# A hybrid decoder block: split float32r products replaced by single float32 products, and the experts' ring filled earlier

## The chip, the cores and the metric

The kernel runs on one core of a Trainium2 chip. The metric is the device time of one execution in microseconds (us). In the views, PE is the matrix engine and PEld its weight loads, DVE the vector engine, ACT the scalar engine, POOL the general-purpose one, and SP the engine whose queue issues most transfers.

## The reference

One decoder block over 16 meta tokens and 512 tokens of width 1024, in float32. Cut to what matters:

```python
u = rms_norm(h, norm_mix_w)                                  # 528 x 1024
q_a, k_a, v_a, f_a, q_h, f_h, i_h, g_h, gate_a, gate_h = split(u @ w_in)
# attention, 8 heads of 64: logit[t,s] = q_t.k_s/8 + c_t - c_s, c = cumsum(log_sigmoid(f_a))
y_a = softmax(masked logits) @ v_a, then @ w_attn_out        # 512 -> 1024
# HGRN2, 8 heads of 128: S_t = diag(f_t) S_{t-1} + k_t v_t^T, o_t = S_t^T q_t
y_h = (rms_norm(o) * sigmoid(g_h)) @ w_hgrn_out              # 1024 -> 1024
h = h + (sigmoid(gate_a) * y_a + sigmoid(gate_h) * y_h) @ w_o
v = rms_norm(h, norm_ffn_w)
# experts: best of 4 groups, best 2 of the 8 experts in it, gate = softmax weights
h = h + sum over chosen experts of gate * ((silu(a) * b) @ w_e_out[e]),  a, b = split(v @ w_e_in[e])
out = rms_norm(h, norm_final_w)[16:]
```

There are 32 experts with 1024 x 1024 weights in and 512 x 1024 out, 201 MB in all, and every one of them is read.

## The kernel before, in words

**Projections.** The normalised input lies transposed in `u`, 8 blocks of 128 rows by 528 columns, and is kept as two float32r tiles, `uh` (the rounded value) and `ul` (what the rounding left). A weight tile of 128 output columns (8 x 128 x 128) is loaded as float32 by `fetch`, half a transfer of 1 MB at a time, and `cut` splits it into `wh` (ACT, line 158) and `wl` (DVE, line 159). `mm3` then makes three products for each of the 8 blocks: `wh` with `uh`, `wh` with `ul`, `wl` with `uh`; the fourth, low with low, is left out. Where the meta tokens are needed (`proj(True)`: forget gate and values of HGRN2, keys and values of attention) the 528 columns are done as two halves of 264; otherwise as 512. The order is: 8 heads of HGRN2 with four tiles each, 8 tiles of `w_gh`, 8 of `w_ho` (on `ohT_h`, `ohT_l`), 4 pairs of attention heads with three tiles each, 8 tiles of `w_ga` (the attention gates), 8 half-long tiles of `w_ao` (on `oaT_h`, `oaT_l`), and `w_o` in `part` (on `mixh`, `mixl`).

**Side work.** After each of the 8 blocks `stage.step()` lets a generator (`hgrn`, `attend`) put its next few instructions between the products, so that scans, softmax and transposes run beside the projections. In `attend` a score block is one product of high parts stacked over 128 rows (line 684) and one of 66 rows that carries the low parts and the forget bias (line 685).

**Transfers.** SP issues its transfers in program order. `weights` asks for loads up to three ahead of the current tile. 16 tiles (`SLOTS`) of a pool serve all big buffers and 5 more (`STREAM`) the weights and their splits. A transfer into a tile waits until the last reader of the tile's previous owner is done, and what follows it on SP waits too.

**Experts.** Experts p and p + 16 make a pair; its weights come as 12 chunks of 1 MB, 192 in all. 18 chunks (`RING`) are kept ahead through `ahead`, two more (`LOOSE`) lie in small buffers. In `first`, rows gathered for the pair (64 for each expert) meet the weights in float32, the two experts in the two halves of the array's columns (line 1126); SiLU; transposes; in `second` the product with the second weights (line 1166). The result `py` is split into `yh` and `yl` (lines 1170, 1171), and `scatter` multiplies both by the one-hot `PT` (lines 1212, 1213), 128x512 each, and adds `gate` times the sum to `x`. The second half of a pair's scatter runs between the transposes and the second product of the next pair (`fill`). Chunks are first asked for in the loop over `w_o`, after its first half.

Of the kernel before, what the change touches and what calls it, by code (L numbers as in the profile page):

```python
# [9 lines left out]
F32R = mybir.dt.float32r  # L10
# [18 lines left out]
SLOTS = 16  # L29
STREAM = 5  # L30
# [7 lines left out]
SHARED = (9, 10, 11, 16, 17)  # L38
# [26 lines left out]
def hybrid_block(tc, I, out, dbg=None):  # L65
# [3 lines left out]
    with ctx:  # L69
# [8 lines left out]
        def slot(name, n=4, dt=F32, w=None, stream=False):  # L78

            t_ = sb.tile([128, SLOT], dt, tag="stream" if stream else "slot", bufs=STREAM if stream else SLOTS, name=name)  # L80
            w = w or {4: L, 2: 1024, 1: 2048}[n]
            return t_[:, :n * w].rearrange("p (n w) -> p n w", n=n)
# [106 lines left out]
        ys, y2, sums, pvs, us = {}, {}, {}, {}, {}  # L189
# [29 lines left out]
        def fa(b):  # L219

            n, _, c0 = rows[b]
            o = pf[b // 2 if b > 0 else 0][:, c0 % 272:c0 % 272 + n]
            for i in range(2):
                for g in range(4):
                    T.matmul(o[32 * g:32 * g + 32], wfa[:, 4 * i + g], us[b, i][:, g], start=(i == 0), stop=(i == 1))

        def sw(b, i):
            n, _, c0 = rows[b]
            u = us[b, i] = slot("u")[:, :, :n]
            V.tensor_tensor(u, pvs[b, i], nmw[:, 4 * i:4 * i + 4, None].to_broadcast([128, 4, n]), op=ALU.mult)  # L230

        def hi(b, i):
            n, _, c0 = rows[b]
            A.activation(uh[i][:, :, c0:c0 + n], us[b, i], AF.Copy)

        def lo(b, i, eng):
            n, _, c0 = rows[b]
            eng.tensor_tensor(ul[i][:, :, c0:c0 + n], us[b, i], uh[i][:, :, c0:c0 + n].bitcast(F32), op=ALU.subtract)

        with tc.manual_schedule(engines={getattr(mybir.EngineType, e) for e in ("PE", "DVE", "Activation", "Pool")}):  # L240
# [23 lines left out]
            hi(-1, 0)  # L264
            hi(-1, 1)
            lo(-1, 0, G)
            lo(-1, 1, G)
# [4 lines left out]
            hi(0, 0)  # L272
            lo(0, 0, G)
            dg(2)
            sw(1, 0)
            ms(3)
            hi(0, 1)
            lo(0, 1, G)
            hi(1, 0)
            fa(0)  # L280
            tr(2, 0)
            lo(1, 0, G)
            cut(0)
            sw(1, 1)
            dg(3)
            tr(2, 1)
            hi(1, 1)
            lo(1, 1, G)
            fa(1)
            sw(2, 0)  # L290
            tr(3, 0)
            sw(2, 1)
            hi(2, 0)
            hi(2, 1)
            tr(3, 1)
            lo(2, 0, G)
            fa(2)
            sw(3, 0)
            sw(3, 1)
            hi(3, 0)  # L300
            hi(3, 1)
            lo(3, 0, G)
            fa(3)
            lo(2, 1, V)
            lo(3, 1, V)
        cut(1)
# [13 lines left out]
        def weights():  # L320
# [1055 lines left out]
```

## Time and profile before

| | us |
|---|---|
| median of 3 runs (1096.1 to 1099.58) | 1098.77 |
| the profiled execution | 1096.76 |
| its span, first to last instruction | 1094.8 |
| PE busy in it | 1047.2 |
| weight loads (PEld) busy | 689.2 |
| DVE busy | 575.0 |
| ACT busy | 329.5 |

Matmuls are pipelined and the ends of their records are modelled, so that a busy PE may still wait for up to the tail of a record. The windows end with the granted clock, the mean busy share of the transfer engines and GB/s. A matmul's form gives the array's part in use (rows * columns) and the moving operand; a float32r matmul is listed as f32 too. A row of the timeline or of the chain with a count covers that many instructions from the first one's start to the last one's end.

### The profile page before, as it was taken

How to read it: one execution, taken by the hardware profiler on the slowest of the kernel's cores; microseconds unless marked ns; L12 is line 12 of the kernel's file. 1: busy time of each engine (PE TensorE's matmuls, PEld its weight loads, DVE VectorE, ACT ScalarE, POOL GpSimd, SP SyncE). 2: the span in 40 equal slices, each digit the busy share in tenths (PEclk: the TensorE clock that was granted, in tenths of full speed). 3: DMA queues.
4: the chain of work that ended last, by engine and by line, in shares of the span. 5: the costliest groups of instructions: out<-in, count | busy, mean ns of one | idle time of the engine just before them, and what ended most of it. 6: DMA issues, size and time to landing. Idle time of an engine off the chain costs nothing.

```text
span 1094.8 us, 16543 instructions
## 1 busy us (share of the span) xinstructions
PE 1047.2 (96%) x6756; PEld 689.2 (63%) x6757; DVE 575.0 (53%) x1269; ACT 329.5 (30%) x643; POOL 67.7 (6%) x88
## 2 busy tenths in 40 slices
PE   9999999999999999999999999999999999988984
PEld 8888988988888898777788634333443333333331
DVE  6967877677633466666653533333443333323324
ACT  5545655555551243344434300000000000000003
POOL 5000000000000121100000000000000000000002
PEclk9999999999999999999999999999999999999997
DMA  6211221121222211221287999999999999999993
GB/s 221 95 44 74 78 78 43 75 79 40 78 86 89 96 59 59 79 77 39 77 323 299 321 419 419 418 419 420 419 418 420 419 419 420 420 420 418 420 415 127
DMA packets 41139, 255.61 MB, mean 233 GB/s; under 512 B 6143, under 2 KB 6399, under 8 KB 12000
## 3 DMA queue, kind: packets, MB, share of 16 engines
q1 hardware_dynamic: 37328, 248.39, 57.3%
q0 software_dynamic: 2416, 3.98, 1.0%
q10 hardware_dynamic: 1312, 2.11, 0.5%
q8 instruction: 55, 0.90, 0.3%
q14 instruction: 28, 0.23, 0.1%
HBM read 254.15 MB, written 4.19 MB: 236 GB/s over the span
## 4 chain that ended last, share of the span: by engine, by line
PE 60%; DMA 32%; DVE 4%; issue 1%; ACT 1%; POOL 0%; DVEq 0%; SPq 0%; ACTq 0%; POOLq 0%
DMA ch<-w_e 30%; PE pj L344 24%; PE py L344 6%; PE pk L344 5%; PE phu L1126 4%; PE pye L1166 4%; PE pd L561 1%; PE ph L1026 1%; PE pu L215 1%; PE ph L1024 1%; PE poa L712 1%; PE ph L1025 1%; PE pout L1212 1%; DMA xslot<-rows_of,xslot 1%; DMA rows_of<-v 1%
## 5 line engine op out<-in xcount | busy, mean ns | idle before, releaser
L344 PE MATMUL pj<-uh,ws 128*128 128x512 f32 (+1 forms) x928 | 295.0, 363 | 1.6 <-DVE ws L159 1.1
L1126 PE MATMUL phu<-ch,xslot 128*64 128x512 f32 x1024 | 232.6, 598 | 20.7 <-DMA ch<-w_e 20.7
L344 PEld LDWEIGHTS pj<-uh,ws 128*128 128x128 f32 x928 | 174.8, 189 | 27.3 <-issue 2.0
L1126 PEld LDWEIGHTS phu<-ch,xslot 128*64 128x64 f32 x1024 | 68.1, 136 | 175.9 <-issue 113.0
L344 PE MATMUL pj<-ul,ws 128*128 128x512 f32 (+1 forms) x464 | 164.1, 354 | 0.0
L1139 DVE TENSOR_TENSOR hs<-hs,phu 128x512 f32<-128x512 f32 x16 | 11.0, 688 | 208.6 <-PE phu L1126 191.4
L159 DVE TENSOR_TENSOR ws<-w,ws 128x1024 fp32r<-128x1024 f32 (+1 forms) x84 | 98.0, 1168 | 34.3 <-ACT ws L158 34.1
L1166 PE MATMUL pye<-ch,hs 128*64 128x512 f32 x512 | 113.9, 596 | 1.6 <-DVE hs L1152 1.1
L158 ACT ACTIVATE ws<-w 128x1024 fp32r<-128x1024 f32 (+1 forms) x83 | 84.2, 1015 | 54.0 <-PE py L344 40.3
L344 PE MATMUL pk<-uh,ws 128*128 128x264 f32 x352 | 95.4, 285 | 0.0
L344 PEld LDWEIGHTS pj<-ul,ws 128*128 128x128 f32 x464 | 87.4, 188 | 9.5 <-issue 0.2
L1214 DVE SCALAR_TENSOR_TENSOR x<-pout,gate,x 128x512 f32<-128x512 f32 x128 | 87.1, 742 | 1.1 <-PE pout L1213 1.1
L1138 ACT ACTIVATE hs<-phu 128x512 f32<-128x512 f32 x16 | 9.6, 597 | 254.6 <-PE phu L1126 254.6
L1166 PEld LDWEIGHTS pye<-ch,hs 128*64 128x64 f32 x512 | 35.1, 137 | 71.5 <-issue 64.6
L1170 ACT ACTIVATE yh<-pye 128x512 fp32r<-128x512 f32 x32 | 19.1, 598 | 163.2 <-PE pye L1166 163.2
L344 PEld LDWEIGHTS pk<-uh,ws 128*128 128x128 f32 x352 | 66.4, 189 | 0.6
L1171 DVE TENSOR_TENSOR yl<-pye,yh 128x512 fp32r<-128x512 f32 x32 | 22.1, 692 | 70.3 <-ACT yh L1170 68.7
L1212 PE MATMUL pout<-yh,PT 128*128 128x512 f32 x128 | 57.0, 445 | 0.0
L1213 PE MATMUL pout<-yl,PT 128*128 128x512 f32 x128 | 50.5, 395 | 0.2 <-DVE yl L1171 0.2
L344 PE MATMUL pk<-ul,ws 128*128 128x264 f32 x176 | 50.0, 284 | 0.0
L1212 PEld LDWEIGHTS pout<-yh,PT 128*128 128x128 f32 x128 | 24.0, 187 | 27.4 <-issue 13.8
L344 PE MATMUL py<-ohh,ws 128*128 128x512 f32 x128 | 40.3, 394 | 0.0
(323 smaller groups left out, 1520.7 us busy)
## 6 DMA issues: line engine op xcount, KB each, us to landing
ch<-w_e SPq DMA_DIRECT2D x189, 1024.0 KB, 20.0
w<-w_h SPq DMA_DIRECT2D x16, 1024.0 KB, 5.1
w<-w_gh SPq DMA_DIRECT2D x4, 1024.0 KB, 4.9
w<-w_ho SPq DMA_DIRECT2D x4, 1024.0 KB, 4.9
w<-w_a SPq DMA_DIRECT2D x4, 1024.0 KB, 5.0
w<-w_ga SPq DMA_DIRECT2D x4, 1024.0 KB, 4.9
w<-w_o SPq DMA_DIRECT2D x4, 1024.0 KB, 4.8
x<-x SPq DMA_DIRECT2D x4, 512.0 KB, 5.2
```

Of the source, the lines that this page charges most:

```text
L158: a = A.activation(wh, w, AF.Copy)
L159: b = V.tensor_tensor(wl, w, wh.bitcast(F32), op=ALU.subtract)
L215: T.matmul(pvs[b, i][:, k], rows[b][1][:, 512 * i + 128 * k:512 * i + 128 * k + 128], dgs[b], start=True, stop=True)
L344: T.matmul(p[i], a[:, k], m(k, i), start=(k == 0 and j == 0), stop=(k == nk - 1 and j == 2))
L1126: T.matmul(ph[n][r], x_[k // 4][:, k % 4, r], w[2 * e + n], start=(k == 0), stop=(k == KD - 1))
L1139: V.tensor_tensor(hs, hs, ph[1], op=ALU.mult)
L1166: T.matmul(py[n][r], hs[:, 128 * k + 64 * e:128 * k + 64 * e + 64], w[2 * (k % 2) + e], start=(k == 0), stop=(k == 3))
L1170: A.activation(yh[n], py[n], AF.Copy)
L1171: V.tensor_tensor(yl[n], py[n], yh[n].bitcast(F32), op=ALU.subtract)
L1212: T.matmul(po, PT[:, tb], yh[n], start=True, stop=False)
L1213: T.matmul(po, PT[:, tb], yl[n], start=False, stop=True)
L1214: V.scalar_tensor_tensor(x[tb][:, c], po, gate[:, tb, p:p + 1], x[tb][:, c], op0=ALU.mult, op1=ALU.add)
```

## The change

Every product of split operands becomes one product of plain float32 operands. `cut`, the high and low tiles and the instructions that make them go. `mm3` (three products) becomes `mm` (one), and the order of the normalisation's steps at the start is rewritten without the splits. A score block is one product of 65 rows: 64 of the head and one for the bias; `X` moves into `Y`'s tile. `scatter` is one product for each of 4 row blocks and half. `part` reads `mix` itself. The two pools of 16 and 5 tiles become one of 21. The chunks' loads begin one each after gates 2 to 8, then one after every second tile of `w_ao`, then the rest of the first 18 in the loop over `w_o`. The branch for experts with more than 64 rows changes in the same way.

```diff
-SLOTS = 16
-STREAM = 5
+SLOTS = 21
-SHARED = (9, 10, 11, 16, 17)
+EARLY = [i for i in range(20) if i not in LOOSE]
...
-            if i < len(loads) and ("l", i) not in made:
-                w = slot("w", 1, stream=True)[:, 0]
-                nc.sync.dma_start(w[:, :loads[i][1]], loads[i][0])
-                made["l", i] = w
-
-        def cut(i):
-            if i >= len(tiles) or ("s", i) in made:
-                return
-            li, o, c = tiles[i]
-            fetch(li)
-            w = made["l", li][:, o:o + c]
-            ws = slot("ws", 2, F32R, stream=True)
-            wh, wl = ws[:, 0, :c], ws[:, 1, :c]
-            if i == 0:
-                V.tensor_copy(wh, w)
-            else:
-                a = A.activation(wh, w, AF.Copy)
-            b = V.tensor_tensor(wl, w, wh.bitcast(F32), op=ALU.subtract)
-            if i == 1:
-                tc.keep_in_program_order(a)
-                tc.keep_in_program_order(b)
-            made["s", i] = [m.rearrange("p (k c) -> p k c", c=128 if c > 256 else 32) for m in (wh, wl)]
+            if i < len(loads) and i not in made:
+                made[i] = slot("w", 1)[:, 0]
+                nc.sync.dma_start(made[i][:, :loads[i][1]], loads[i][0])
...
-        uh = [slot(f"uh{i}", 4, F32R) for i in range(2)]
-        ul = [slot(f"ul{i}", 4, F32R) for i in range(2)]
+        u = [slot(f"u{i}", 4) for i in range(2)]
...
         def sw(b, i):
             n, _, c0 = rows[b]
-            u = us[b, i] = slot("u")[:, :, :n]
-            V.tensor_tensor(u, pvs[b, i], nmw[:, 4 * i:4 * i + 4, None].to_broadcast([128, 4, n]), op=ALU.mult)
-
-        def hi(b, i):
-            n, _, c0 = rows[b]
-            A.activation(uh[i][:, :, c0:c0 + n], us[b, i], AF.Copy)
-
-        def lo(b, i, eng):
-            n, _, c0 = rows[b]
-            eng.tensor_tensor(ul[i][:, :, c0:c0 + n], us[b, i], uh[i][:, :, c0:c0 + n].bitcast(F32), op=ALU.subtract)
+            V.tensor_tensor(u[i][:, :, c0:c0 + n], pvs[b, i], nmw[:, 4 * i:4 * i + 4, None].to_broadcast([128, 4, n]),
+                            op=ALU.mult)
...
-            fetch(tiles[i][0])
-            cut(i)
+            li, o, c = tiles[i]
+            fetch(li)
             if i + 1 < len(tiles):
                 for j in range(AHEAD + 1):
                     fetch(tiles[i + 1][0] + j)
-                cut(i + 1)
-            return made.pop(("s", i))
-
-        def mm3(p, wh, wl, mh, ml, nk, apart=False):
-
-            if apart:
-                for i in range(len(p)):
-                    for j, (a, m) in enumerate(((wh, mh), (wl, mh), (wh, ml))):
-                        for k in range(nk):
-                            T.matmul(p[i], a[:, k], m(k, i), start=(k == 0 and j == 0), stop=(k == nk - 1 and j == 2))
-                return
-            for ii in [range(len(p))]:
+            w = made[li][:, o:o + c]
+            if i + 1 == len(tiles) or tiles[i + 1][0] > li:
+                made[li] = None
+            return w.rearrange("p (k c) -> p k c", c=128)
+
+        def mm(p, w, m, nk, apart=False):
+
+            for i in range(len(p)) if apart else (0,):
                 for k in range(nk):
-                    for j, (a, m) in enumerate(((wh, mh), (wh, ml), (wl, mh))):
-                        for i in ii:
-                            T.matmul(p[i], a[:, k], m(k, i), start=(k == 0 and j == 0), stop=(k == nk - 1 and j == 2))
-                    stage.step()
+                    for j in (i,) if apart else range(len(p)):
+                        T.matmul(p[j], w[:, k], m(k, j), start=(k == 0), stop=(k == nk - 1))
+                    if not apart:
+                        stage.step()
 
         def proj(full):
-            wh, wl = weights()
+            w = weights()
             if full:
-                n = wh.shape[-1]
-                p = [bank("pj", True)[:n], bank("pk", True)[:n]]
-                mm3([a[:, 0:264] for a in p], wh, wl, lambda k, i: uh[k // 4][:, k % 4, 264 * i:264 * i + 264],
-                    lambda k, i: ul[k // 4][:, k % 4, 264 * i:264 * i + 264], KD, state["n"] <= 2)
-                return [a[:, 0:264] for a in p]
+                p = [bank("pj", True)[:, 0:264], bank("pk", True)[:, 0:264]]
+                mm(p, w, lambda k, i: u[k // 4][:, k % 4, 264 * i:264 * i + 264], KD, state["n"] <= 2)
+                return p
             p = bank("pj", True)
-            mm3([p], wh, wl, lambda k, i: uh[k // 4][:, k % 4, M:], lambda k, i: ul[k // 4][:, k % 4, M:], KD)
+            mm([p], w, lambda k, i: u[k // 4][:, k % 4, M:], KD)
...
-            V.scalar_tensor_tensor(oo, pt, hnw, g, op0=ALU.mult, op1=ALU.mult)
-            A.activation(ohT_h[h // 4][:, h % 4], oo, AF.Copy)
-            V.tensor_tensor(ohT_l[h // 4][:, h % 4], oo, ohT_h[h // 4][:, h % 4].bitcast(F32), op=ALU.subtract)
+            V.scalar_tensor_tensor(ohT[h // 4][:, h % 4], pt, hnw, g, op0=ALU.mult, op1=ALU.mult)
...
-                        T.matmul(p_[:, :n], X[h][0][:, r], Y[:, 2 * h, kk], start=True, stop=False)
-                        T.matmul(p_[:, :n], X[h][1][0:66, r], Y[0:66, 2 * h + 1, kk], start=False, stop=(k0 + n <= P))
+                        T.matmul(p_[:, :n], X[h][0:65, r], Y[0:65, h, kk], start=True, stop=(k0 + n <= P))
...
-            Y = slot("Y", 4, F32R)
-            X = [[piece(f"X{h}{j}", F32R, S) for j in range(2)] for h in range(2)]
+            Y = slot("Y", 4)
+            X = [Y[:, 2 + h, :S] for h in range(2)]
             for h in range(2):
                 r = slice(64 * h, 64 * h + 64)
-                nc.gpsimd.dma_start(Y[64:66, 2 * h + 1], chl[2 * pr + h:2 * pr + h + 1])
-                V.tensor_scalar(X[h][1][64:66], mhalf[64:66, 0:1].to_broadcast([2, S]), 2.0, None, op0=ALU.mult)
-                both(lambda o, i_: A.activation(o, i_[r], AF.Copy), Y[0:64, 2 * h], pk)
-                for i in range(2):
-                    o = slice(264 * i, 264 * i + 264)
-                    V.tensor_tensor(Y[0:64, 2 * h + 1, o], pk[i][r], Y[0:64, 2 * h, o].bitcast(F32), op=ALU.subtract)
-                G.tensor_copy(Y[64:128, 2 * h], Y[0:64, 2 * h].bitcast(F32))
+                nc.gpsimd.dma_start(Y[64:65, h], cfs[2 * pr + h:2 * pr + h + 1])
+                V.tensor_scalar(X[h][64:65], mhalf[64:65, 0:1].to_broadcast([1, S]), 2.0, None, op0=ALU.mult)
+                both(lambda o, i_: A.activation(o, i_[r], AF.Copy), Y[0:64, h], pk)
             pq = proj(False)
             for h in range(2):
-                r = slice(64 * h, 64 * h + 64)
-                A.activation(X[h][0][0:64], pq[r], AF.Copy, scale=0.125)
-                V.scalar_tensor_tensor(X[h][0][64:128], pq[r], 0.125, X[h][0][0:64].bitcast(F32), op0=ALU.mult, op1=ALU.subtract)
-                G.tensor_copy(X[h][1][0:64], X[h][0][0:64].bitcast(F32))
+                A.activation(X[h][0:64], pq[64 * h:64 * h + 64], AF.Copy, scale=0.125)
...
             logistic(ga[d], [pg])
+            if d:
+                ahead(EARLY[d - 1])
         stage.drain()
         if dbg:
-            nc.sync.dma_start(dbg["oa"], oaT_h.bitcast(F32))
-        mhl = [slot(f"mhl{b}", 2, F32R) for b in range(NB)]
-        mixh, mixl = ([m[:, j].rearrange("p (d t) -> p d t", d=KD) for m in mhl] for j in range(2))
+            nc.sync.dma_start(dbg["oa"], oaT)
         for d in range(KD):
-            wh, wl = weights()
+            w = weights()
             p = bank("py", True)
-            mm3([p], wh, wl, lambda k, i: oaT_h[:, k], lambda k, i: oaT_l[:, k], 4)
+            mm([p], w, lambda k, i: oaT[:, k], 4)
             g, t = ga[d], mix[d // 4][:, d % 4]
             V.tensor_tensor(g, p, g, op=ALU.mult)
             V.tensor_tensor(t, t, g, op=ALU.add)
-            for b in range(NB):
-                tt = t[:, 128 * b:128 * b + 128]
-                A.activation(mixh[b][:, d], tt, AF.Copy)
-                V.tensor_tensor(mixl[b][:, d], tt, mixh[b][:, d].bitcast(F32), op=ALU.subtract)
+            if d % 2:
+                ahead(EARLY[7 + d // 2])
...
-            cc = slice(512 * (k % 2), 512 * (k % 2) + 512)
-            a, b_ = (z_.rearrange("p k c -> p (k c)")[:, cc] for z_ in ab)
-            mh, ml = mixh[tb][:, k], mixl[tb][:, k]
-            T.matmul(p, mh, a, start=(k == 0), stop=False)
-            T.matmul(p, ml, a, start=False, stop=False)
-            T.matmul(p, mh, b_, start=False, stop=(k == KD - 1))
+        def part(p, tb, k, w):
+            T.matmul(p, mix[k // 4][:, k % 4, 128 * tb:128 * tb + 128],
+                     w.rearrange("p k c -> p (k c)")[:, 512 * (k % 2):512 * (k % 2) + 512],
+                     start=(k == 0), stop=(k == KD - 1))
...
-            for i in (*range(6), 8, 9, 10):
+            for i in EARLY[11:14]:
...
-            for i in (11, 12, 13):
+            for i in EARLY[14:16]:
...
-                ahead(tb + 13)
                 normal(tb - 1)
                 route(tb - 1)
 
             tb = NB - 1
-            ahead(tb + 14)
-            for i in (18, 19):
+            for i in EARLY[16:]:
...
-                A.activation(yh[n], py[n], AF.Copy)
-                V.tensor_tensor(yl[n], py[n], yh[n].bitcast(F32), op=ALU.subtract)
+                A.activation(y[n], py[n], AF.Copy)
...
-            PT, yh, yl = Y[p]
+            PT, y = Y[p]
             c = slice(512 * n, 512 * n + 512)
             for tb in range(NB):
                 po = bank("pout")
-                T.matmul(po, PT[:, tb], yh[n], start=True, stop=False)
-                T.matmul(po, PT[:, tb], yl[n], start=False, stop=True)
+                T.matmul(po, PT[:, tb], y[n], start=True, stop=True)
                 V.scalar_tensor_tensor(x[tb][:, c], po, gate[:, tb, p:p + 1], x[tb][:, c], op0=ALU.mult, op1=ALU.add)
```

## Rows read from the trace of the kernel before

**Rows 1.** The page's 40 slices: PE's busy tenths, and what transfers moved.

```profile
PE   9999999999999999999999999999999999988984
...
GB/s 221 95 44 74 78 78 43 75 79 40 78 86 89 96 59 59 79 77 39 77 323 299 321 419 419 418 419 420 419 418 420 419 419 420 420 420 418 420 415 127
```

**Rows 2.** Windows: length; busy us (count) of PE, PEld, DVE, ACT, POOL; clock; transfers.

```profile
33.00:618.10 585.10, 581.09 (x4424) 494.73 (x4424) 370.85 (x880) 271.56 (x537) 30.81 (x39) 1.00 0.29 100
618.10:1094.80 476.70, 436.12 (x2045) 166.67 (x2044) 179.94 (x332) 39.10 (x73) 23.05 (x23) 0.99 0.97 399
...
672.90:699.50 26.60, 26.60 (x130) 10.61 (x130) 10.79 (x20) 1.79 (x3) 0.99 (x1) 1.00 1.01 418
726.00:1062.00 336.00, 314.79 (x1463) 117.67 (x1464) 120.82 (x210) 19.72 (x33) 9.89 (x10) 1.00 1.01 419
```

**Rows 3.** PE's waits from 33.0 to 618.1: us, times, longest; six entries.

```profile
PE prk L872 <- DVE ob L866: 1.6, 3, 0.7
PE pj L344 <- DVE ws L159: 1.1, 1, 1.1
...
```

**Rows 4.** The chain in order of time: start, us, what.

```profile
300.56 22.94 PE pj L344 x99
323.51 44.80 PE py L344 x192
```

**Rows 5.** Timeline of SP's queue before the experts: the chunks' loads.

```profile
555.76 54.98 SPq L928 DMA_DIRECT2D ch<-w_e  x18
```

**Rows 6.** PE's groups by form: count, busy us, mean ns of one.

```profile
L1126 PE MATMUL phu<-ch,xslot 128*64 128x512 f32 x1024 | 232.6, 598 | 20.7 <-DMA ch<-w_e 20.7
L344 PE MATMUL pj<-uh,ws 128*128 128x512 f32 x576 | 198.2, 404 | 1.6 <-DVE ws L159 1.1 <-issue 0.5
...
L344 PE MATMUL pk<-uh,ws 128*128 128x264 f32 x352 | 95.4, 285 | 0.0
...
L225 PE MATMUL pf<-u,wfa 128*32 128x128 f32 x64 | 2.6, 279 | 0.0
```

**Rows 7.** Timeline: the second pair's first product, and one step's weight loads.

```profile
646.13 13.95 PE L1126 MATMUL phu<-ch,xslot 128*64 128x512 f32 x64
646.61 0.14 PEld L1126 LDWEIGHTS phu<-ch,xslot 128*64 128x64 f32 x2 [0.28 <-issue]
```

**Rows 8.** Timeline of PE at the start.

```profile
18.50 0.86 PE L225 MATMUL pf<-u,wfa 128*32 128x128 f32 x24
...
19.30 0.39 PE L338 MATMUL pj<-uh,ws 128*128 128x264 f32 x1
...
28.73 2.13 PE L338 MATMUL pk<-uh,ws 128*128 128x264 f32 x16
...
33.39 0.73 PE L344 MATMUL pj<-uh,ws 128*128 128x512 f32 x2 [1.10 <-DVE ws L159]
```

**Rows 9.** The page's costliest groups: two of DVE.

```profile
L159 DVE TENSOR_TENSOR ws<-w,ws 128x1024 fp32r<-128x1024 f32 (+1 forms) x84 | 98.0, 1168 | 34.3 <-ACT ws L158 34.1
...
L1214 DVE SCALAR_TENSOR_TENSOR x<-pout,gate,x 128x512 f32<-128x512 f32 x128 | 87.1, 742 | 1.1 <-PE pout L1213 1.1
```

**Rows 10.** Timeline of DVE at the start.

```profile
14.01 1.23 DVE L159 TENSOR_TENSOR ws<-w,ws 128x1024 fp32r<-128x1024 f32 x1
```

**Rows 11.** Timeline of PE in the second pair: scatter's groups and what follows them.

```profile
661.40 0.48 PE L1212 MATMUL pout<-yh,PT 128*128 128x512 f32 x1
...
663.73 7.09 PE L1166 MATMUL pye<-ch,hs 128*64 128x512 f32 x32
670.75 0.51 PE L1212 MATMUL pout<-yh,PT 128*128 128x512 f32 x1
...
672.79 0.65 PE L1126 MATMUL phu<-ch,xslot 128*64 128x512 f32 x2
```

**Rows 12.** Timeline of PE at the end: the last pair's second product, in two pieces.

```profile
1067.08 5.37 PE L1166 MATMUL pye<-ch,hs 128*64 128x512 f32 x24
...
1073.96 1.94 PE L1166 MATMUL pye<-ch,hs 128*64 128x512 f32 x8
```

More of the change, by code (lines that the diff above doesn't have):

```diff
@@ L76, in st, with slot @@
             return sb.tile(shape, dt, tag=tag or name, bufs=bufs, name=name or tag)
-        def slot(name, n=4, dt=F32, w=None, stream=False):
-            t_ = sb.tile([128, SLOT], dt, tag="stream" if stream else "slot", bufs=STREAM if stream else SLOTS, name=name)
+        def slot(name, n=4, dt=F32, w=None):
+            t_ = sb.tile([128, SLOT], dt, tag="slot", bufs=SLOTS, name=name)
             w = w or {4: L, 2: 1024, 1: 2048}[n]
@@ L391, in hybrid_block @@
         V.tensor_tensor_scan(cf, zero1[:8].to_broadcast([8, L]), z, 0.0, op0=ALU.add, op1=ALU.add)
-        chl = inside(cc, 2 * L, F32R).rearrange("p (j t) -> p j t", j=2)[0:8]
-        V.tensor_copy(chl[:, 0], cf)
-        V.tensor_tensor(chl[:, 1], cf, chl[:, 0].bitcast(F32), op=ALU.subtract)
+        cfs = inside(cc, L)[0:8]
+        V.tensor_copy(cfs, cf)
         if dbg:
@@ L407, in hybrid_block @@
         V.tensor_scalar(lb[:, 1], lb[:, 0], -1.0, 1.0, op0=ALU.mult, op1=ALU.add)
-        ohT_h = [slot(f"ohh{i}", 4, F32R, S) for i in range(2)]
-        ohT_l = [slot(f"ohl{i}", 4, F32R, S) for i in range(2)]
+        ohT = [slot(f"oh{i}", 4, F32, S) for i in range(2)]
         sT = [inside(ca, S).rearrange("p (c t) -> p c t", c=NB) for i in range(2)]
@@ L628, in hybrid_block @@
             for i in range(2):
-                nc.sync.dma_start(dbg["ohn"][i], ohT_h[i].bitcast(F32))
+                nc.sync.dma_start(dbg["ohn"][i], ohT[i])
         for d in range(KD):
-            wh, wl = weights()
+            w = weights()
             p = bank("py", True)
-            mm3([p], wh, wl, lambda k, i: ohT_h[k // 4][:, k % 4], lambda k, i: ohT_l[k // 4][:, k % 4], KD)
+            mm([p], w, lambda k, i: ohT[k // 4][:, k % 4], KD)
             V.tensor_tensor(mix[d // 4][:, d % 4], p, mix[d // 4][:, d % 4], op=ALU.mult)
-        oaT_h, oaT_l = slot("oah", 4, F32R, S), slot("oal", 4, F32R, S)
+        oaT = slot("oa", 4, F32, S)
         def attend(pr, X, Y, v):
@@ L717, in attend @@
                             T.matmul(po[hd[h], c0:c0 + n], vm[:, hd[h]], pt_[h][:M, o:o + n], start=False, stop=False)
-            A.activation(oaT_h[:, pr], po, AF.Copy)
-            V.tensor_tensor(oaT_l[:, pr], po, oaT_h[:, pr].bitcast(F32), op=ALU.subtract)
+            A.activation(oaT[:, pr], po, AF.Copy)
             yield
@@ L745, in hybrid_block, with place_of, ahead @@
             stage.add(attend(pr, X, Y, v_))
+        chunks = {}
+        def place_of(i):
+            return i - sum(j < i for j in LOOSE)
+        def ahead(i):
+            if i < 12 * NP and i not in chunks:
+                if i in LOOSE:
+                    chunks[i] = [piece(f"ch{j}", F32, S) for j in range(4)]
+                    for j in range(4):
+                        nc.sync.dma_start(chunks[i][j], I["w_e"][i][:, 512 * j:512 * j + 512])
+                    return
+                w = slot("ch", 1)[:, 0]
+                for h in ([slice(0, 1024), slice(1024, 2048)] if i == 12 * NP - 1 else [slice(0, 2048)]):
+                    nc.sync.dma_start(w[:, h], I["w_e"][i][:, h])
+                chunks[i] = [w[:, 512 * j:512 * j + 512] for j in range(4)]
         ga = [piece(f"ga{d}", F32, S, d < KEEP) for d in range(KD)]
@@ L763, in hybrid_block @@
             V.tensor_tensor(t, t, g, op=ALU.add)
-            for b in range(NB):
-                tt = t[:, 128 * b:128 * b + 128]
-                A.activation(mixh[b][:, d], tt, AF.Copy)
-                V.tensor_tensor(mixl[b][:, d], tt, mixh[b][:, d].bitcast(F32), op=ALU.subtract)
+            if d % 2:
+                ahead(EARLY[7 + d // 2])
         if dbg:
-            for b in range(NB):
-                nc.sync.dma_start(dbg["mixed"][b], mixh[b].bitcast(F32))
+            for b in range(2):
+                nc.sync.dma_start(dbg["mixed"][b], mix[b])
         wbr = piece("wbr", keep=True)
@@ L911, in count @@
             V.tensor_copy(extrai[:, 32:33], extra[:, 1, 0:1])
-        chunks = {}
-        def place_of(i):
-            return i - sum(j < i for j in LOOSE)
-        def ahead(i):
-            if i < 12 * NP and i not in chunks:
-                if i in LOOSE:
-                    chunks[i] = [piece(f"ch{j}", F32, S) for j in range(4)]
-                    for j in range(4):
-                        nc.sync.dma_start(chunks[i][j], I["w_e"][i][:, 512 * j:512 * j + 512])
-                    return
-                w = slot("ch", 1, stream=place_of(i) % RING in SHARED)[:, 0]
-                for h in ([slice(0, 1024), slice(1024, 2048)] if i == 12 * NP - 1 else [slice(0, 2048)]):
-                    nc.sync.dma_start(w[:, h], I["w_e"][i][:, h])
-                chunks[i] = [w[:, 512 * j:512 * j + 512] for j in range(4)]
         def chunk(i):
@@ L1033, in hybrid_block @@
         for kk in range(4):
-            ab = weights()
+            w = weights()
             for tb in range(NB):
                 for k in (2 * kk, 2 * kk + 1):
-                    part(pp[tb], tb, k, ab)
+                    part(pp[tb], tb, k, w)
         stage.drain()
@@ L1155, in second @@
             back(p)
-            yh = [piece(f"yh{n}", F32R, S) for n in range(2)]
-            yl = [piece(f"yl{n}", F32R, S) for n in range(2)]
-            Y[p] = [J.pop(p)["PT"], yh, yl]
+            y = [piece(f"y{n}", F32, S) for n in range(2)]
+            Y[p] = J.pop(p)["PT"], y
             py = [bank("pye", True) for _ in range(2)]
@@ L1311, in hybrid_block @@
                                 po = bank("pox")
-                                T.matmul(po, PT[:, tb], yh, start=True, stop=False)
-                                T.matmul(po, PT[:, tb], yl, start=False, stop=True)
+                                T.matmul(po, PT[:, tb], yx, start=True, stop=True)
                                 V.scalar_tensor_tensor(x[tb][:, c], po, gcol[:, tb:tb + 1], x[tb][:, c],
```

48 lines of the change are left out of this document (11 added, 37 removed).

## Prediction

> **What bounds the kernel now.** I read the page's slices first [rows 1]: PE reads 9 nearly to the end, but the transfers sit at 40 to 100 GB/s for most of twenty slices and then climb to 420. So there are two stages with different limits. The windows price them [rows 2]: from 33.0 to 618.1 us PE is busy 581.1 of 585.1 us; from 618.1, where the experts start, the transfers run at 399 GB/s on average. A busy PE can still be waiting inside its records' modelled ends, so I took the list of waits in the first stage [rows 3]: six entries for PE, 4.5 us in all. That stage is a string of products on PE, and nothing else ends a wait there for long. In the chain [rows 4] its dense stretches price one streamed product of 512 columns: 22.94 us for 99 and 44.80 for 192, 0.2325 each.
>
> In the second stage the ring's 18 loads were issued over 55 us from 555.8 us on [rows 5], just ahead of the experts. While it lasts PE does a pair of experts in 26.6 us [rows 2]. Twelve loads of 1.0486 MB at 419 GB/s take 30.0, so once the lead is used up the transfers set the pace: from 726 on PE is busy 314.8 of 336 us [rows 2], and more of its waiting hides inside modelled ends.
>
> **The unknown: one float32 product on the whole array.** No row shows a plain float32 product of 512 columns on 128x128. What is shown: a plain product leaves two matmul records (512 products in line 1126, 1024 records [rows 6]), a split one leaves one. In line 1126 two neighbouring 64-column tiles of the array work; 64 records take 13.95 us, and the weight loads come in twos [rows 7]. With 0.60 for the last record [rows 6], two records start every (13.95 - 0.60) / 31 = 0.431 us. Either the two run side by side and each streams its 512 columns twice, or they run one after the other and stream them once. The forget-gate product decides: 24 records of 128 columns on four 32-column tiles take 0.86 us [rows 8], 0.28 of it the last one's duration [rows 6], so five steps of 0.116 for four records each. Streamed once, 128 columns cost 0.2325 x 128 / 512 = 0.058 us: four side by side would take 0.058, one after another 0.232. Twice and side by side gives 0.116, which is the measurement. The durations say the same: 598 ns against 404 for a split product of 512 columns [rows 6], longer by about one streaming.
>
> A plain product is thus two records of two streamings each. I take 0.431 us for a 512-column record on the whole array, from the row that is nearest in type and columns. Lower bound: streamed once, 0.2325. Upper bound: a split product costs 0.2325 where half of 0.431 is 0.2155, 1.079 times as much; if whole-array weights are the reason, a plain record costs 0.465.
>
> **Projections.** Three records become two of about twice the length. By the code there are 36 tiles with 512 columns and eight products each (the 576 records with the high operand [rows 6] are two of three), 8 x 8 products of w_ho, 8 x 4 of w_ao and 64 of w_o: 448. The 24 tiles over all 528 columns give 16 products of 264 each: 384.
> - 512 columns: 2 x 0.431 = 0.862 against 3 x 0.2325 = 0.697; 448 x 0.165 = +73.9 us.
> - 264 columns: before, 16 records in 2.13 us [rows 8] with 0.285 for the last [rows 6], 0.123 each, 0.369 for three; after, 0.431 x 264 / 512 = 0.222, 0.444 for two; 384 x 0.075 = +28.8 us.
>
> Together +102.7 us, all of it on the engine that bounds this stage.
>
> **Scores.** Lines 684 and 685 each stream 144 + 272 + 400 + 528 columns for each of 8 heads, 10752; one plain product takes their place. Two streamings at 0.2325 / 512 come to 9.8 us, four at 0.431 / 1024 to 18.1: +8.3 us.
>
> **What is taken off DVE, ACT and POOL.** The low halves alone cost DVE 98.0 us [rows 9], yet PE waited for them 1.1 us after the start [rows 3]. Much work goes and little time: what hides it is PE's own string of products, and that only grows. The copies of X and Y between partitions and the halves of ohT, oaT and mix go the same way, at nothing. At the start they do count. One split of 1.23 us stands on DVE ahead of the last normalised blocks [rows 10]; and from 19.30, where the first projection begins, to 33.39, where the third really gets going after a wait for ws, 14.1 us pass [rows 8] for 96 x 0.123 + 2 x 0.2325 = 12.3. That is 1.2 + 1.8 us, and with the other short waits I take -5; the far end is -15, since idle time under a modelled end isn't listed.
>
> The experts then start at 618.1 + 102.7 + 8.3 - 5 = 724 us.
>
> **Scatter.** Each pair has two groups of four products, each of them two split records now. The group behind the second product runs from 670.75 to 672.79, 2.04 us; the one between the transposes and the second product from 661.40 to 663.73, 2.33 [rows 11]. Four plain products take 4 x 0.862 = 3.45: +1.41 and +1.12, so +2.5 us a pair, and 26.6 becomes 29.1. The subtraction of yl is hidden behind the other multiplies already, except in the last pair. DVE adds each product to x in 0.742 us [rows 9], still under 0.862, so it doesn't take over.
>
> **The ring, filled from the gates on.** Eleven of the first 18 loads move ahead of the loop over w_o. That buys little: the ring was nearly full at 618 us before as well. On SP's queue they move past loads of w_ga, w_ao and w_o, which then stand behind any chunk that waits for a slot. These are asked for three loads ahead, at least five tiles of up to 6.9 us each; I cost the move at nothing with that cover, and where it goes, PE waits for a late load.
>
> With a full ring the experts take PE's time or the transfers', whichever is longer. PE's before, without waits for chunks: 28.0 us for the first pair (618.1 to 646.13 [rows 7]), 14 x 26.6, and for the last 17.6 up to its second product (646.13 to 663.73, as in [rows 7, 11]) and 27.7 from there (1067.08 [rows 12]) to the end: 446. After: 446 + 1.4 + 15 x 2.5 = 485. Transfers: 174 chunks at 2.5 us, 435, and 20.8 from the last chunk's multiply at 1073.96 [rows 12] to the end: 456. PE is later: 485 against 476.7 before, +8.
>
> **Sum**, against the profiled execution, 1096.8 us with a span of 1094.8 and 2 outside it: 724 + 485 + 2 = **1211 us**. The median of the runs shown, 1098.8, lies 2 above the profiled one and within their spread of 3.5; I leave 1211.
>
> **Rivals.**
> - *Whole-array records are slower, 0.465.* For: split products show the 8%. Against: line 1126 streams the same type without it. Projections 448 x 0.233 + 384 x 0.110 = +147, scores +9.8, a scatter group 3.72, so +3.1 a pair and experts 446 + 1.7 + 46 = 494: 618 + 157 - 5 + 494 + 2 = 1266.
> - *Scatter is hidden* because the transfers stay the limit. For: 29.1 a pair on PE is just under their 30.0. Against: a full ring is 45 us of lead. Experts 456 to 461: 1182 to 1187.
> - *SP's queue blocks.* A chunk that waits for attention's slots holds up w_ao or w_o. Two to four loads that each stand behind two chunks, 7.5 us: 1226 to 1241. For: 18 chunks need slots while attention holds four or five and weights four. Against: cc, x, u, mix and oa hold eight, so I count 21 of 21 at the sixth gate and fewer when attention is drained.
> - *Faster: whole-array records stream once*, and weight loads set the pace, two in place of three. Projections go to 0.465 and 0.246 a product, -448 x 0.232 - 384 x 0.123 = -151; scores and scatter stay. The experts start at 462 and are bound by the transfers, 461: 925. It decides wherever a 512-column record costs less than about 0.33 us. For: weight loads are busy 494.7 of 585.1 us [rows 2]. Against: [rows 7, 8], which two streamings fit and one doesn't.
>
> The Trainium skill, Perfetto Trace Analysis, section Identifying the Most-Contended Engine, says that matmul busy time is a poor measure of how near PE is to its limit, since products are pipelined, and that the share of weight loads is a better one. By that rule a third fewer loads would count most, which is the side of the last rival; here loads read 85% of the first stage, below the products' 99%. The Trainium skill, FP8 and Floating Point Precision, section TensorE Precision Notes, speaks against it: true float32 takes four passes through the array. No row here shows that on the whole array.
>
> **Chances.** Forecast, 1190 to 1240: 0.73. Slower records: 0.12. SP blocked: 0.06. Scatter hidden: 0.05. Streamed once: 0.04, of which 0.01 ends near no change. The range reaches from the hidden scatter, 1187, to 1255, into the slower records. About 0.3%, 3 us, is what a measurement of this kernel tells from no change: faster 0.03, same 0.01, slower 0.96.
>
> **What would show it.** Two records per product in the projections' line, 0.43 us apart at 512 columns and 0.22 at 264; the first expert product near 724 us; pairs of experts at an even 29 us, with no PE wait for chunks and the transfers somewhat below 419 GB/s; chunk loads around the gates and no PE wait for w. The prediction fails if whole-array records come 0.23 us apart (faster) or 0.46 and more, or if PE waits for a weight load behind a chunk.

## The result, and the profile after

The changed kernel takes 1214.4 us, median of 4 runs (1212.8 to 1215.1), against 1098.5 before (1096.1 to 1099.6): 1.106 times, 95% interval 1.1035 to 1.1078, slower. The profiled execution took 1212.8 with a span of 1211.0 us. The forecast was 1211, within 1187 to 1255.

The page of the changed kernel, its totals and its 40 slices (the same lines as in [rows 1]):

```profile
PE 1190.0 (98%) x5924; PEld 620.4 (51%) x5925; DVE 441.1 (36%) x1081; ACT 242.9 (20%) x510; POOL 42.0 (3%) x64
...
PE   9999999999999999999999999999999999999994
...
GB/s 332 58 71 36 36 70 71 71 3 68 139 105 18 0 53 35 70 140 104 104 250 104 104 210 411 420 419 419 419 419 419 418 419 419 419 419 419 419 256 72
```

DVE and ACT lost 220 us of work between them, the matmul records fell from 6756 to 5924 and the weight loads from 63% of the span to 51%; the time rose. The Trainium skill, Perfetto Trace Analysis, section Identifying the Most-Contended Engine, has PE's headroom judged by the busy share of weight loads, beside the share of peak arithmetic. By the weight loads PE has more room than before; the measurement decides otherwise. The transfers reach 411 GB/s in the 25th slice, right behind the experts' start at 719.8 us, as they reach 419 in the 24th of [rows 1].

PE's groups by form, changed kernel (against [rows 6]):

```profile
L287 PE MATMUL pj<-u,w 128*128 128x512 f32 x576 | 261.5, 595 | 0.0
L1048 PE MATMUL phu<-ch,xslot 128*64 128x512 f32 x1024 | 223.5, 594 | 0.0
L1132 PE MATMUL pout<-y,PT 128*128 128x512 f32 x256 | 116.9, 599 | 0.0
L287 PE MATMUL pj<-u,w 128*128 128x264 f32 x384 | 115.1, 388 | 0.0
```

Whole-array plain records now stand in the trace: two for each product, with the duration that the 64-column ones had. Their spacing is in the timeline. First the start (against [rows 8]), then the eight tiles of w_ho, then the experts' first product and their third pair (against [rows 7] and [rows 11]):

```profile
19.46 3.83 PE L287 MATMUL pj<-u,w 128*128 128x264 f32 x16
23.13 3.72 PE L287 MATMUL pk<-u,w 128*128 128x264 f32 x16
...
33.81 6.60 PE L287 MATMUL pj<-u,w 128*128 128x512 f32 x15
...
372.19 55.10 PE L287 MATMUL py<-oh,w 128*128 128x512 f32 x128
...
719.77 3.65 PE L1048 MATMUL phu<-ch,xslot 128*64 128x512 f32 x16
...
778.71 13.95 PE L1048 MATMUL phu<-ch,xslot 128*64 128x512 f32 x64
...
794.06 3.60 PE L1132 MATMUL pout<-y,PT 128*128 128x512 f32 x8
797.59 7.09 PE L1087 MATMUL pye<-ch,hs 128*64 128x512 f32 x32
804.60 3.70 PE L1132 MATMUL pout<-y,PT 128*128 128x512 f32 x8
808.24 1.08 PE L1048 MATMUL phu<-ch,xslot 128*64 128x512 f32 x4
```

With 0.592 us for the last one, 128 records of w_ho give (55.10 - 0.59) / 127 = 0.429 us each, and 264 columns (3.72 - 0.39) / 15 = 0.222. A pair of experts takes 808.24 - 778.71 = 29.5 us. The windows show both stages with next to no idle time on PE (against [rows 2]; columns as there):

```profile
33.80:719.80 686.00, 685.50 (x3627) 417.92 (x3625) 252.16 (x689) 191.80 (x416) 14.78 (x23) 1.00 0.22 80
749.30:1162.50 413.20, 413.20 (x1790) 153.16 (x1790) 138.74 (x235) 25.07 (x42) 12.86 (x13) 1.00 1.01 419
```

SP's queue around the gates (against [rows 5]):

```profile
526.03 5.67 SPq L691 DMA_DIRECT2D ch<-w_e  x2
...
564.35 0.80 SPq L691 DMA_DIRECT2D ch<-w_e  x2
...
645.14 0.33 SPq L142 DMA_DIRECT2D w<-w_o  x1
645.51 65.55 SPq L691 DMA_DIRECT2D ch<-w_e  x7
```

The first two chunks go out at 526, nine more in ones and twos between weight loads, and seven only between 645 and 711 us. The queue did wait for tiles. Its list of waits has, for chunks that waited for w_o's products (us, times, longest):

```profile
SPq L691 <- PE ph L948: 42.4, 3, 16.3
```

PE's own list of waits is empty from 33 to 719.8 us: it never waited for w.

Where the time went, by the first product of each stretch (from the start of its first record to that of the next, us; from the timeline of either kernel):

| stretch | before | after | difference |
|---|---|---|---|
| up to the first projection | 19.3 | 19.5 | +0.2 |
| HGRN2's tiles and w_gh | 304.0 | 352.7 | +48.7 |
| w_ho | 44.8 | 54.9 | +10.1 |
| attention's tiles and w_ga | 161.2 | 190.3 | +29.1 |
| w_ao | 22.5 | 27.5 | +4.9 |
| w_o, routing | 66.1 | 74.9 | +8.7 |
| experts to the end | 476.8 | 491.2 | +14.4 |

### The profile page after: what moved, and what is told of

It is laid out like the page before. It is cut to its first block, busy times and chain, and to the rows that moved or that the text cites. A ratio compares the mean times of both kernels' runs of the same rounds, so it can differ in the third digit from the quotient of the medians.

```text
span 1211.0 us, 14469 instructions
## 1 busy us (share of the span) xinstructions
PE 1190.0 (98%) x5924; PEld 620.4 (51%) x5925; DVE 441.1 (36%) x1081; ACT 242.9 (20%) x510; POOL 42.0 (3%) x64
## 5 line engine op out<-in xcount | busy, mean ns | idle before, releaser
L287 PE MATMUL pj<-u,w 128*128 128x512 f32 (+1 forms) x960 | 374.8, 512 | 0.0
L287 PEld LDWEIGHTS pj<-u,w 128*128 128x128 f32 x960 | 174.0, 190 | 120.6 <-issue 109.1
L1132 PE MATMUL pout<-y,PT 128*128 128x512 f32 x256 | 116.9, 599 | 0.0
L287 PE MATMUL pk<-u,w 128*128 128x264 f32 x384 | 114.6, 386 | 0.0
L287 PEld LDWEIGHTS pk<-u,w 128*128 128x128 f32 x384 | 73.0, 190 | 12.4
L1132 PEld LDWEIGHTS pout<-y,PT 128*128 128x128 f32 x256 | 46.0, 190 | 59.7 <-issue 55.1
L948 PE MATMUL ph<-w,mix 128*128 128x512 f32 x128 | 57.2, 595 | 0.0
L287 PE MATMUL py<-oh,w 128*128 128x512 f32 x128 | 55.1, 592 | 0.0
L287 PEld LDWEIGHTS py<-oh,w 128*128 128x128 f32 x128 | 24.3, 190 | 30.6 <-issue 30.6
L948 PEld LDWEIGHTS ph<-w,mix 128*128 128x128 f32 x128 | 23.5, 190 | 25.3 <-issue 25.3
L633 ACT ACTIVATE pa<-s,mx 128x400 f32<-128x400 f32 (+3 forms) x40 | 19.1, 482 | 58.3 <-DVE mx L629 30.6
```

Of the source, the lines that this page charges most:

```text
L287: T.matmul(p[j], w[:, k], m(k, j), start=(k == 0), stop=(k == nk - 1))
L633: A.activation(ps_[h][:, k0:k0 + n], p_[:, :n], AF.Exp, bias=mx[:, 0:1], accum_out=mx[:, 2 + jj:3 + jj])
L948: T.matmul(p, mix[k // 4][:, k % 4, 128 * tb:128 * tb + 128], w.rearrange("p k c -> p (k c)")[:, 512 * (k % 2):512 * (k % 2) + 512], start ...
L1132: T.matmul(po, PT[:, tb], y[n], start=True, stop=True)
```

## The experiments

The theory: the time is PE's streamings, in the first stage always and in the experts' stage wherever PE needs more than the transfers; the splits were hidden, the early ring buys next to nothing. Each kernel below undoes or does one part. The kernel before was timed beside each of them, with medians from 1097.0 to 1098.5 us, so 1 to 2 us between two of the changed kernels tell nothing.

**The ring, late again.** The changed kernel, with the chunks asked for as before.

```diff
-            if d:
-                ahead(EARLY[d - 1])
...
-            if d % 2:
-                ahead(EARLY[7 + d // 2])
...
-            for i in EARLY[11:14]:
+            for i in EARLY[0:9]:
...
-            for i in EARLY[14:16]:
+            for i in EARLY[9:12]:
...
+                ahead(tb + 13)
...
-            for i in EARLY[16:]:
+            for i in (17, 18, 19):
```

> The changed kernel with the ring of chunks asked for only from the loop over w_o on, in the order of the kernel before; all products stay plain. Theory (the time is PE's products; the ring has lead enough either way): within 3 us of the changed kernel, 1211 to 1218 us, and pairs of experts still 29.5 us apart with no PE wait for chunks; at most a few us of waits in the last pairs, because the last chunk would land about 456 us after the experts start and PE needs it 470 us after. Rival (the early ring is what keeps PE fed): pairs go to 30.0 us once the lead is gone and the time rises by 8 us or more, to 1222 or above.

1215.2 us (1.107 times before, 1.105 to 1.109), 0.8 above the changed kernel, which is within the noise; the pairs stay at 29.5 us. SP's queue in this kernel, timeline:

```profile
626.65 86.60 SPq L691 DMA_DIRECT2D ch<-w_e  x18
713.35 13.22 SPq L687 DMA_DIRECT2D ch<-w_e  x8
726.66 32.31 SPq L691 DMA_DIRECT2D ch<-w_e  x14
```

The 18 loads start 100 us later than in the changed kernel (626.65 against 526.03) and still are all issued by 713, before the experts start at 722. The early ring is worth nothing here.

**The scatter, split again.** The changed kernel with `yh`, `yl` and two products in `scatter`; the tiles `PT`, `yh` and `yl` are float32r again.

```diff
-                A.activation(y[n], py[n], AF.Copy)
+                A.activation(yh[n], py[n], AF.Copy)
+                V.tensor_tensor(yl[n], py[n], yh[n].bitcast(F32), op=ALU.subtract)
...
-                T.matmul(po, PT[:, tb], y[n], start=True, stop=True)
+                T.matmul(po, PT[:, tb], yh[n], start=True, stop=False)
+                T.matmul(po, PT[:, tb], yl[n], start=False, stop=True)
```

> The changed kernel with the scatter alone back as two split products; projections, scores and ring stay as changed. Theory (plain scatter makes PE the limit of the experts' stage): PE needs 26.7 us a pair again, the transfers' 30.0 take over after the lead, the stage takes about 456 to 463 us in place of 491, the time 1178 to 1188 us. Rival 1 (scatter was hidden under the transfers all along): 1211 to 1217 us. Rival 2 (the transfers don't matter at all, PE alone counts): 16 x 2.9 us less, 1166 to 1170 us.

1198.1 us (1.0915, 1.0895 to 1.0934), 16.4 less than the changed kernel's 1214.4 (the experts' stage 475.2 against 491.2 in the traces), but outside each of the three bands. PE's waits, from 620 to 1180 us:

```profile
PE phu L1049 <- DMA ch<-w_e: 20.1, 37, 0.8
```

The transfers did take over, as the theory has it, after nine pairs (27.8 us the first, 26.7 the others); only their stage is 475 us long and not 456 to 463. My price for them was wrong; the section on the prediction says in what.

**Both.** Late ring and split scatter together, the two edits above.

> The changed kernel with both undone, the late ring and the split scatter, so that only projections and scores are plain. Theory: the experts' stage is that of the kernel before, about 477 us, behind a first stage of 720: 1195 to 1201 us, and the difference to the kernel with split scatter alone is what filling the ring early is worth where transfers bind, some 10 to 18 us. Rival (the early ring is worth nothing, since SP's queue was blocked for most of it): no difference to split scatter alone, both at 1195 or both at 1180.

1197.6 us (1.0915, 1.0896 to 1.0934): no difference to the split scatter alone, so the rival of this run holds: the early ring is worth nothing even where transfers bind. The windows ahead of the experts, first with the early ring, then with the late one (columns as in [rows 2]):

```profile
660.00:690.00 30.00, 30.00 (x93) 14.88 (x92) 2.76 (x4) 4.14 (x11) 0.00 (x0) 1.00 0.19 70
...
720.00:730.00 10.00, 8.89 (x58) 4.01 (x58) 4.59 (x20) 2.75 (x6) 1.13 (x1) 1.00 1.00 327
730.00:740.00 10.00, 8.75 (x50) 3.54 (x46) 4.09 (x13) 0.60 (x1) 0.79 (x1) 1.00 1.01 415
```

```profile
640.00:660.00 20.00, 20.00 (x48) 8.89 (x47) 2.77 (x4) 0.00 (x0) 0.00 (x0) 1.00 0.96 400
660.00:690.00 30.00, 30.00 (x97) 15.23 (x96) 2.77 (x4) 4.14 (x11) 0.00 (x0) 1.00 0.19 70
...
720.00:730.00 10.00, 8.89 (x53) 3.11 (x54) 5.55 (x25) 2.38 (x5) 1.14 (x1) 1.00 0.89 325
```

Both are at 70 GB/s from 660 to 690, since SP's queue waits for tiles that are still being read (its waits for w_o's products: 42.5 us with the early ring). When the chunks are asked for makes no difference; that their room, 18 chunks and 2, is what counts is my reading, for no run changed it. From the start of the experts both need the same 475 us.

**The kernel before with the plain scatter alone.**

```diff
-                T.matmul(po, PT[:, tb], yh[n], start=True, stop=False)
-                T.matmul(po, PT[:, tb], yl[n], start=False, stop=True)
+                T.matmul(po, PT[:, tb], y[n], start=True, stop=True)
```

> The kernel before with the scatter alone made plain. Theory: the first stage stays at 618 us, PE becomes the limit of the experts' stage at 29.5 us a pair, 491 us: 1110 to 1114 us, 12 to 16 above the kernel before. Rival (hidden under the transfers): 1097 to 1100 us. Rival (PE's added 46 us all count): 1140 us or more.

1113.5 us (1.0153, 1.0129 to 1.0178), 15.6 above the kernel before, timed beside it. The window over nearly all of the middle fourteen pairs (columns as in [rows 2], where from the fifth pair on PE was busy 314.8 of 336 us):

```profile
648.00:1060.00 412.00, 412.00 (x1786) 152.93 (x1787) 137.59 (x234) 25.07 (x42) 12.85 (x13) 1.00 1.01 419
```

PE has no gap left; 29.5 us a pair, 490.6 for the stage against 476.8. So the scatter's price is shown from both sides, 16.4 us out of the changed kernel and 15.6 into the old one, and neither rival holds: it isn't hidden, nor do all of PE's 46 us count.

**The weight splits' work put back.** The changed kernel; the same shapes on ACT and DVE for every weight tile, without use.

```diff
+        def again(i):
+            if i < len(tiles) and ("s", i) not in made:
+                li, o, c = tiles[i]
+                w = made[li][:, o:o + c]
+                A.activation(w, w, AF.Copy)
+                V.tensor_tensor(w, w, w, op=ALU.max)
+                made["s", i] = True
...
+            for j in (i, i + 1):
+                again(j)
```

> The changed kernel with the weights' former work put back without its use: each weight tile is copied onto itself on ACT and then combined with itself on DVE before its products (some 84 instructions of 1.0 us and 84 of 1.2 us), so the products get the same numbers as without. Theory (the split work was hidden behind PE's products except at the start): 0 to 5 us above the changed kernel, 1214 to 1220 us. Rival (taking the split work off DVE and ACT gave back 8 us or more of hidden stalls): 1222 us or above, spread over the first stage.

1219.5 us (1.1119, 1.1101 to 1.1138), 5.1 above the changed kernel, inside the first band, at its edge. Timeline of PE at the start, and PE's wait for it in the list (the only other one, in w_o, is 0.2 us):

```profile
25.33 5.27 PE L298 MATMUL pj<-u,w 128*128 128x264 f32 x16 [5.52 <-DVE w L274]
30.43 3.72 PE L298 MATMUL pk<-u,w 128*128 128x264 f32 x16
```

```profile
PE pj L298 <- DVE w L274: 5.5, 1, 5.5
```

It is lost in the first half of the first projection: its first record is 5.9 us late and it takes 1.4 us longer (5.27 against 3.83), since here the first two tiles' work on DVE, at 24.07 us, stands behind that engine's steps for attention's forget gates. From the second half on (30.43 against 23.13, 7.3 us late) to the experts (727.5 against 719.8, 7.7) another 0.4 us comes in 700. The span grows by 5.9 us and not by 7.7, because the last pair's second product is followed by 19.8 us here and 21.6 in the changed kernel; over all traces of this case that end takes 19.8 to 22.2. Some 180 us of work on two engines (96 on DVE, 83 on ACT) cost next to nothing under PE's products.

**The ring earlier in the kernel before.** Its first four chunks asked for in the loop over w_ao; `ahead` is defined earlier for it.

```diff
+            if d % 2:
+                ahead(d // 2)
```

> The kernel before with only the ring's first four chunks asked for during w_ao's loop, after every second tile; all products stay split. Theory (there the transfers bind the experts' stage, so loads moved ahead of it count): the last chunk lands up to four chunks earlier, 4 x 2.5 us: 1086 to 1094 us, 4 to 12 below the kernel before. Rival (the ring's tiles, not the time of asking, limit it): within 3 us of the kernel before, 1096 to 1100 us. Rival (SP's queue holds up w_o behind a chunk): above 1100 us with PE waits for w.

1097.4 against 1097.0 us timed beside it (1.0001, 0.999 to 1.0011). Windows of this kernel, then of the kernel before (columns as in [rows 2]):

```profile
530.00:556.00 26.00, 26.00 (x113) 20.89 (x112) 23.36 (x56) 14.39 (x44) 0.31 (x3) 1.00 0.54 207
556.00:618.00 62.00, 59.82 (x347) 50.28 (x345) 26.73 (x89) 23.32 (x44) 2.22 (x4) 1.00 0.74 273
```

```profile
530.00:556.00 26.00, 25.92 (x112) 20.27 (x111) 23.98 (x57) 13.68 (x41) 0.35 (x3) 1.00 0.27 89
556.00:618.00 62.00, 60.02 (x349) 50.65 (x347) 26.17 (x88) 24.00 (x48) 2.22 (x4) 1.00 0.90 340
```

What comes earlier is missing later, 207 GB/s in place of 89 and then 273 in place of 340, and the experts' stage is the same, 476.6 against 476.8. The rival holds, as in the runs with split scatter.

**The kernel before with the plain scores alone.** The tiles `X` and `Y` and the single row for the bias are those of the changed kernel.

```diff
-                        T.matmul(p_[:, :n], X[h][0][:, r], Y[:, 2 * h, kk], start=True, stop=False)
-                        T.matmul(p_[:, :n], X[h][1][0:66, r], Y[0:66, 2 * h + 1, kk], start=False, stop=(k0 + n <= P))
+                        T.matmul(p_[:, :n], X[h][0:65, r], Y[0:65, h, kk], start=True, stop=(k0 + n <= P))
```

> The kernel before with attention's scores alone as single plain products (65 rows, X inside Y's tile, the bias in one row); projections, scatter and ring as before. Theory (the streamed columns count in full): the attention stretch, from the first product behind w_ho to the first of w_ao, grows from 161.2 us by 8 us, the time by 7 to 9 us. Rival (about half is given back, because four split steps per head pair and the copies between partitions go and the wait for softmax shrinks): the stretch grows by 3 to 5 us and so does the time. Rival (hidden): 0 to 2 us.

1101.9 us (1.0044, 1.003 to 1.0058), 4.3 more; the stretch grows from 161.2 to 165.8, by 4.5. The middle reading fits. Part of it is my price: by the starts of the records all split pairs of the scores take 12.1 us before and the plain products 19.0, +6.9 and not +8.3, mostly because split records of 128 and 144 columns take 0.10 to 0.115 us on average to the next start, not the 0.058 to 0.065 that streaming alone would. The other 2.4 us were given back around them: 1.0 us is the waits of the transposes for the softmax, ptr 0.6 and ptm 0.4 in the kernel before's list, which have no entry here; where the rest went stays open.

**The kernel before with w_ho alone plain.** The weights are still split, without use for these eight tiles; `w` is the float32 tile and `ohT` one float32 tile in place of two.

```diff
-            mm3([p], wh, wl, lambda k, i: ohT_h[k // 4][:, k % 4], lambda k, i: ohT_l[k // 4][:, k % 4], KD)
+            for k in range(KD):
+                T.matmul(p, w[:, k], ohT[k // 4][:, k % 4], start=(k == 0), stop=(k == KD - 1))
+                stage.step()
```

> The kernel before with the 64 products of w_ho alone as plain products; the weight tiles are still split as before, without use for these eight. Theory (two records of 0.429 us in place of three of 0.2325, nothing hides them): 64 x 0.161 = 10.3 us in the stretch from the first w_ho product to the first of attention (44.8 to 55 us) and 9 to 12 us in the time. Rival (one streaming per record, the change's loss comes from elsewhere): the stretch falls to 30 us, the time by 15.

1108.9 us (1.0096, 1.0081 to 1.0111), 11.3 more. The timeline (44.8 us in [rows 4]):

```profile
324.14 55.10 PE L632 MATMUL py<-oh,w 128*128 128x512 f32 x128
```

The stretch takes 54.5 us up to the next product, 9.7 more, and the time follows in full. One streaming per record, the rival, is out.

**Two gates with one streaming.** The kernel before with the tiles of w_gh and w_ga as one product of the rounded operands; the products with low parts are left out there.

```diff
+        def gate_proj():
+            wh, wl = weights()
+            p = bank("pj", True)
+            for k in range(KD):
+                T.matmul(p, wh[:, k], uh[k // 4][:, k % 4, M:], start=(k == 0), stop=(k == KD - 1))
+                stage.step()
+            return p
```

> The kernel before with the 16 tiles of the two merge gates (w_gh, w_ga) as one product of the rounded operands in place of three; the two products with low parts are left out for these tiles, so the gates are less exact. Theory (the first stage is the count of streamings): 128 x 2 x 0.2325 = 59.5 us less in the first stage, the experts' stage unchanged at 477 us, 1035 to 1042 us. Rival (the side work becomes the bound where products shrink to a third: logistic's two passes, and attention's last softmax, which drains inside w_ga's tiles): 10 to 25 us of PE waits in these two stretches and 1048 to 1065 us.

1050.2 us (0.9567, 0.9553 to 0.9581): below both kernels, with less exact gates. The first stage is 48.1 us shorter, 618.1 to 569.9, not 59.5; the time lies in the rival's range. PE's waits in the first stage (4.5 us in all before [rows 3]), the first five:

```profile
PE py L344 <- ACT ws L158: 2.2, 2, 1.8
PE pj L363 <- ACT ws L158: 2.0, 3, 0.9
PE prk L880 <- DVE ob L874: 1.4, 3, 0.6
PE pj L344 <- DVE ws L159: 1.1, 1, 1.1
PE po L590 <- ACT ca L583: 1.0, 1, 1.0
```

Four fifths of the count came through; the splits and the side work now end waits. The list's thirteen entries add up to 11.2 us, 6.7 more than before. By the stretches of the table above, 6.9 of the missing 11.4 us lie between the first projection and the end of w_ho, and 4.7 between there and the end of w_ao, where the end of attention's work now runs behind w_ao's first product. A part of the loss is not named by the list and stays open.

## Why the prediction was right, and where its terms were off

- **Two streamings per record on the whole array**: right. It was taken from products on 64 and 32 columns; the whole array gave 0.429 and 0.222 us against 0.431 and 0.222. A product takes 2 x 0.429 us, so a streaming 0.2145. The rival of slower records is out: plain records on the whole array have whole-array weights and show no sign of the 8% that split ones carry (0.2325); what makes those 8% stays open. The Trainium skill, FP8 and Floating Point Precision, section TensorE Precision Notes, states that true float32 takes four passes through the array. The trace agrees, with two records of two streamings.
- **First stage**: the experts start at 719.8, forecast 724. w_ho gave +10.1 where 64 x 0.165 is 10.6, and +9.7 alone. The scores were mis-sized, +8.3 against 4.5 measured alone: short split records aren't paid by their columns, and waits went with them. w_o and the routing gave +8.7 where 64 x 0.165 is 10.6; waits of 1.9 us that the kernel before has there are gone.
- **The splits hidden**: right, shown for the weights' by putting their 180 us back; the rest of the 220 us taken off DVE and ACT was not put back. At the start, where 3 of the 5 us were placed (1.2 + 1.8), the term was too large: the first projection begins at 19.46 and not earlier, since PE's transposes of the last block run from 16.27 us and ran from 16.55 before; only the 1.8 us of waiting behind it went. What made the -5 come out about right lies elsewhere: all six waits of [rows 3], 4.5 us with the 1.1 for ws that belongs to the 1.8, are gone from PE's list.
- **Scatter**: 29.5 us a pair against 29.1, and 491 against 485 for the stage. Four plain products take 3.5 us from the transposes to the second product (794.06 to 797.59) as forecast, 3.64 behind the second product (804.60 to 808.24) where I had 3.45; the rest lies in the 15.35 us from 778.71 to 794.06, 15.27 before.
- **The sum**: 1211 against 1212.8 in the profiled execution is closer than its terms, and that is luck: the first stage came out 4 us shorter than forecast, the experts' stage 6 longer.
- **PE later than the transfers**: right, but by less than thought. The transfers' 456 us should have been 476: I added 174 chunks, 435 us, to the start of the experts as if nothing else moved and all of it at full rate. In the kernel before the last chunk was multiplied 455.9 us after the start, and 20.8 after that is its own 476.7. Once the lead is used up a pair takes 30.6 us and not 30.0, for the gathered rows share the transfers: 3.98 MB (the page's queue q0) over 15 pairs are 0.27 MB beside 12.58, and 12.85 MB at 419 GB/s make 30.7. Over the stage these rows are 9.5 of the missing 20.9 us; the first 28 us, at 369 GB/s in place of 419, are another 3.4; the rest stays open. The rival with the hidden scatter would thus have ended near 1200, not 1187.
- **Transfers somewhat below 419 GB/s**: wrong. They run at 419 in the window from 749 to 1162 us: PE's 29.5 us a pair is shorter than the chunks' 30.6, so the lead shrinks by 1.1 us a pair and the queue never rests.
- **The ring worth little, SP's cover holding**: right; nothing, in three pairs of runs.

## What to carry to other kernels

On a stage that a string of matrix products sets, count streamings times columns and read one streaming's price from the same trace, at a width near the one in question; work taken off other engines pays only where a wait for it ends last, and can be tested by putting equal work back without use. A price can be carried from a tiled product to the whole array if a second tile width tells "side by side" from "one after the other". Where buffers are full before the consumer starts, asking for them earlier moved nothing, in three pairs of runs.

## What the hardware showed that I had not expected

In the scores of the kernel before a split record of 128 or 144 columns costs up to 0.115 us, as much as 253 columns would by the price of long ones. So a plain product costs less than its count of streamings says on short blocks, more so than on long ones: 19.0 against 12.1 us in the scores, 1.57 times for twice the streamings, and 0.858 against 0.699 us for a product of 512 columns, 1.23 times for four streamings in place of three. And transfers held 419 GB/s over 413 us beside a PE without a gap (749.3 to 1162.5), with the same spacing of products as in the first stage at 80 GB/s, 0.43 us: the transfers did not slow the products. Whether they would run faster beside an idle PE no run shows.
